# Memory's keys and values in an order written by hand, with one row of square sums per head; in prompt attention, maxima ahead of key scaling and queries ahead of keys

## The chip, the cores and the metric

The kernel is one program on one NeuronCore of a Trainium2 chip. The metric is the device time of one execution in microseconds (us); the time before is the median of three runs. The engines are named as in the profile: PE is TensorE's matmul, PEld its weight load, DVE is VectorE, ACT is ScalarE, POOL is GpSimd, SP is SyncE, which here only issues DMAs.

## The reference

One step of a decoder layer for two groups of requests, 1024 prompt tokens and 8 samples of 4 tokens, all in 32-bit floats:

```python
u, v, cq, ckv, kpe = split_in(rms_norm(x, g_mix) @ w_in)
a_out = chunk_gmlp(u, v, ...)                    # group A of the mixer
q = qk_rope(rms_norm(rms_norm(cq) @ w_uq))       # group B: 8 heads, 64 + 32 wide
k, vv = keys and values of the latents ckv_n     # prompt: own tokens; samples: 4096 cached ones
b_out = masked softmax attention of q over k, vv
x = x + concat(rms_norm(a_out), rms_norm(b_out)) @ w_o

hm = rms_norm(mem_prompt, g_mem_in)              # 256 memory tokens of 1024
mk = rms_norm((hm @ w_mk) per head of 128, g_mk) # 4 heads; an output of its own
mv = hm @ w_mv                                   # an output of its own
x = x + memory attention of x over mk, mv
x = x + conv_ffn(rms_norm(x))
```

## The kernel before

Everything is kept transposed, features on the 128 partitions and tokens along the row. A product of two 32-bit operands is made of three fast matmuls: each operand is split into a high part (a cast, usually on ACT, line 200 or 204 of `split`) and a low part (the remainder, usually on DVE, line 201 or 207), and `mm3` (line 185) sums high·high, low·high and high·low.

The program runs its stages one after the other: projections, prompt attention (`phase2a`), attention of the samples over cached pages (`phase2b`), memory's keys and values (`mem_kv`), output projection (`mixed`, `out_proj`), memory attention, feed-forward. Where a stage is inside a "manual schedule" of an engine, that engine runs its instructions in the order in which the code is written; elsewhere a scheduler orders them. `behind(a, b)` places instruction a after b.

**Prompt attention.** A unit is one head and one group of query tokens. `head_prep` transposes a head's keys and queries on PE (tiles `tp`) and splits them into `kTh`, `kTl` and `qTh`, `qTl`, 512 tokens at a time; `kT` holds 1024 tokens, in two halves written by two such preparations. `head_unit` takes scores (tiles `s`), their maxima on DVE (`pr`, `nm`), the exponential on ACT, transposes of the exponentials on PE and the sum over values (`o`). Rows of more than 512 keys are scored in two parts, the first over the first half of the row's keys. The scaling of the second 512 keys by their norms is two DVE instructions of `proj_group` (line 960).

**Memory's keys and values.** The raw memory tokens lie in two page buffers (`ck`). Before head 0, eight casts make their high parts `mh` and eight remainders `ml`. Four heads of keys follow (PSUM tile `b`, copies `kr`, squares `sq`), then values over four blocks of `w_mv` (PSUM tiles `v`). Sums over features, which normalise tokens and keys, are 12 matmuls with one column of ones:

```python
for h in range(4):
    for i in range(2):
        nc.tensor.matmul(st[:, 2 * h + i : 2 * h + i + 1], sq[h][:, i * P : i * P + P], self.ones[:, :1], ...)
```

The roots `r` then have a token per partition; to scale the keys they are spread over the partitions by eight matmuls, each of ones with a diagonal matrix that DVE makes of the identity (`diag`, lines 1657 and 1658). Between these lie the last softmax steps of the eighth sample batch (`batch_softmax`, list `late`; its roots are partly on POOL) and its sum over the cached values (`quad_pv`, tiles `o<-ck,S`).

**Output projection.** `mixed` loads `w_o` blocks and the mixer's outputs (`mix`, three chunks of 384, 384 and 288 tokens, split into `mx0`, `mx1`, `mx2`) through one ring of three `raw` buffers; `chunk(m, c)` multiplies block m of `w_o` with chunk c, adds the residual (`res`), stores it, and splits it into `xh`, `xl`, whose memory was that of `mem_kv`. `end` multiplies the samples' attention output `olT` by `w_uv`, and `mixed_sample` normalises it (`n`). SP issues the loads and stores of this stage in one queue.

Of the kernel before, what the change touches and what calls it, by code (L numbers as in the profile page):

```python
# [5 lines left out]
F32 = mybir.dt.float32  # L6
# [147 lines left out]
class Net:  # L154
# [83 lines left out]
    def rsqrt_steps(self, p, out, ss, scale, e=None, eps=EPS):  # L238
# [5 lines left out]
        x, q, y, a = (self.t(p, [P, n], d, f"rq{k}{n}", 2 if n < 100 else 1)[:w] for k, d in (("x", F32), ("h", F32), ("y", I32), ("a", F32)))  # L244
# [5 lines left out]
        for k in range(2):  # L250
            yield
            o = out if k else y
            if e is nc.vector:
# [6 lines left out]
                e.scalar_tensor_tensor(o, q, 5.0, y, ALU.add, ALU.mult)  # L260
# [411 lines left out]
    def phase2a(self):  # L672
# [80 lines left out]
        extra[2][:0] = preps[0][2:]  # L753
# [27 lines left out]
        with tc.manual_schedule(engines={E.PE, E.Activation, E.DVE, E.Pool}):  # L781
# [208 lines left out]
    def head_unit(self, p, pp, h, G, s, c):  # L990
# [7 lines left out]
        def scores(e):  # L998
# [9 lines left out]
            for z in range(nc_):  # L1008
# [3 lines left out]
                self.mm3(sv, [(qh[:, tq], ql[:, tq])], [(kh[:, kc], kl[:, kc])])  # L1012
# [166 lines left out]
    def phase2b(self):  # L1179
# [50 lines left out]
        at(last - 4, 3, lambda: self.split(*wk0, raws[0].rearrange("p (k n) -> p k n", k=8)))  # L1230
        for b in range(NB):
# [3 lines left out]
            for r, (k, pos) in enumerate(((12, 0), (13, 0), (14, 0), (14, 3) if b == NB - 1 else (15, 0), (15, 0) if b == NB - 1 else (15, 3), (16, 0), (17, 0), (17, 3), (18, 2), (19, 2), (20, 0), (21, 2), (22, 3))):  # L1235
                f = lambda b=b, r=r: self.batch_softmax(p, ppt, st[b], r, b == NB - 1)
                if n + k <= last:
                    at(n + k, pos, f)
                else:
                    late.append(f)  # L1240
# [15 lines left out]
        def steps(n0, n1):  # L1256
            for n in range(n0, n1):
# [27 lines left out]
                if 0 <= n < last:  # L1285
                    rope = (Q + 1, quads[Q + 1], st[(Q + 1) // 8]) if n % 2 and Q + 1 < NB * 8 else None
                    for f in self.pair_score(p, pp, n, quads[n // 2], st[n // 16], rope):
                        at(n + 1, -1, f)
# [12 lines left out]
        with tc.manual_schedule(engines={E.SP}):  # L1301
# [5 lines left out]
            mem = self.mem_kv(raws, wk0)  # L1307
            for f in late[:3]:
                f()
            next(mem)  # L1310
            steps(last + 1, last + 4)
            for _ in range(5):
                next(mem)
            steps(last + 4, last + 7)
            for f in late[3:]:
                f()
            for _ in range(6):
                next(mem)
            steps(last + 7, last + 16 + LAG)
            for _ in mem:  # L1320
                pass
# [140 lines left out]
    def batch_softmax(self, p, pp, s, r, final):  # L1462
# [28 lines left out]
        elif r == 4:  # L1491
            s["m"] = self.t(p, [P, 2, 32], F32, "mx", 2)
            peak(0, 0, 24)
        elif r == 5:
            s["it"] = norms(24, 32, nc.gpsimd if final else nc.vector)
# [6 lines left out]
        elif r == 8:  # L1502
            scale(nc.vector, 24, 32)
# [10 lines left out]
        elif r == 11:  # L1514
# [4 lines left out]
            if final:  # L1519
                self.less(nc.vector, s)  # L1520
# [20 lines left out]
    def batch_out(self, p, s, part, pp=None, final=False):  # L1541
        nc = self.nc
        if part == 0:
            s["oo"] = self.t(p, [P, 257], F32, "oo", 2)
            nc.scalar.copy(s["oo"], s["o"])
# [33 lines left out]
    def mem_kv(self, raws, wk0):  # L1579
# [7 lines left out]
        mh, ml = (self.t(p, [P, 8, 256], FR, x) for x in ("mh", "ml"))  # L1587
        acc = [self.t(p, [P, 256], F32, f"acc{z}") for z in range(2)]
        mr = [r.rearrange("p (k n) -> p k n", k=4) for r in raws[1:3]]
        xs = [(mh[:, k], ml[:, k]) for k in range(8)]  # L1590
        kr, sq = [], []

        for h in range(4):
            w = wk0 if h == 0 else self.stream(I["w_mk"][h], 8, raw=raws[3].rearrange("p (k n) -> p k n", k=8) if h == 1 else None)
            if h == 1:
                self.behind(self.cast, cast)
            yield
            ps = self.t(pp, [P, 512], F32, "b", 2)[:, :256]
            pairs = ((0, 0), (1, 0)), ((0, 1),)
            for z in pairs if h == 0 else (((0, 0), (0, 1)), ((1, 0),)):  # L1600
                for k in range(8):
                    if h == 0 and z is pairs[0]:
                        cast = self.split(*xs[k], mr[k // 4][:, k % 4], self.col("g_mem_in", k))
                    for a, e in z:
                        nc.tensor.matmul(
                            ps, w[a][:, k], xs[k][e], start=z[0] == (0, 0) and a + e + k == 0, stop=len(z) == 1 and k == 7
                        )
                    if h == 0 and z is pairs[0] and k % 2:
                        yield
# [988 lines left out]
```

## Time and profile before

| | us |
|---|---|
| three runs | 1813.99, 1815.08, 1815.76 |
| their median | 1815.08 |
| the profiled execution's own time | 1815.49 |
| its span (first to last instruction) | 1813.8 |
| PE busy in it | 1791.1 (99%) |
| DVE, ACT, POOL busy | 1347.4, 921.0, 705.9 |

Some 1.7 us lie outside the span. PE is busy nearly throughout, so a time is to be sought in PE's instructions and in the few places where it waits or runs at its lower clock.

### The profile page before, as it was taken

To read this page: it belongs to the slowest core of one execution; us is meant where nothing else is said; L and a number is where in the kernel's file an instruction comes from. 1 tells how busy PE (TensorE), PEld (TensorE's weight loads), DVE (VectorE), ACT (ScalarE), POOL (GpSimd) and SP (SyncE) were. 2 spreads that over 40 slices of the span, in tenths; PEclk is the share of its full clock that TensorE was granted. 3 is DMA by queue.
4 is the path that set the end of the run, shared out by engine and by line. 5 is a ranking of instruction groups with operands and counts; after the bars stand their busy time and mean duration, and the time that the engine had idled before them with its cause. 6 is when DMAs were issued, how large, how long until landed. Compare 5 with 4: busy or idle time off the path is not lost.

```text
span 1813.8 us, 39386 instructions
## 1 busy us (share of the span) xinstructions
PE 1791.1 (99%) x14259; PEld 1696.6 (94%) x14259; DVE 1347.4 (74%) x2778; ACT 921.0 (51%) x1931; POOL 705.9 (39%) x858
## 2 busy tenths in 40 slices
PE   9999999999999999999999999999999999999999
PEld 8999777769999999998899989999999999999999
DVE  7864777667678777787644678988888888878664
ACT  7335676766556555565434567433333333344442
POOL 1021656534455445453033001476677767400000
PEclk9999999999999999999999999999999999999999
DMA  8101354558876666663655255122222222584242
GB/s 324 48 18 62 118 184 129 164 164 229 226 206 191 190 186 194 178 190 125 188 157 195 97 169 181 58 95 83 72 71 83 72 83 83 163 319 150 88 147 78
DMA packets 153044, 261.06 MB, mean 144 GB/s; under 512 B 20881, under 2 KB 97394, under 8 KB 152850
## 3 DMA queue, kind: packets, MB, share of 16 engines
q1 hardware_dynamic: 151986, 257.50, 45.8%
q8 instruction: 113, 1.85, 0.5%
q10 hardware_dynamic: 864, 1.05, 0.2%
q14 instruction: 81, 0.66, 0.1%
HBM read 212.66 MB, written 45.82 MB: 143 GB/s over the span
## 4 chain that ended last, share of the span: by engine, by line
PE 77%; DVE 5%; ACT 2%; DMA 1%; issue 1%; POOL 1%; SPq 1%; DVEq 0%; ACTq 0%; POOLq 0%
PE s L185 22%; PE d L185 12%; PE b L185 8%; PE E L185 7%; PE F L185 7%; PE X L185 7%; PE A L185 3%; PE o L1046 2%; PE o L1537 2%; PE tp L1031 1%; PE tp L185 1%; PE s L1422 1%; PE tp L984 1%; PE v L185 1%; PE t L185 0%
## 5 line engine op out<-in xcount | busy, mean ns | idle before, releaser
L185 PE MATMUL s<-w2h,ch 128*128 128x256 f32 x1018 | 302.1, 297 | 0.0
L185 PE MATMUL s<-w2h,cl 128*128 128x256 f32 x1018 | 293.6, 288 | 0.0
L185 PE MATMUL s<-w2l,ch 128*128 128x256 f32 x1018 | 293.1, 288 | 0.0
L185 PEld LDWEIGHTS s<-w2h,ch 128*128 128x128 f32 x1018 | 191.6, 188 | 3.3 <-issue 2.9
L185 PEld LDWEIGHTS s<-w2h,cl 128*128 128x128 f32 x1018 | 191.4, 188 | 0.4 <-DVE rqa L257 0.4
L185 PEld LDWEIGHTS s<-w2l,ch 128*128 128x128 f32 x1018 | 191.8, 188 | 0.0
L1458 DVE TENSOR_REDUCE ss<-sq 128x16 f32<-128x1024 f32 x128 | 155.2, 1213 | 29.2 <-ACT sq L1455 29.1
L1407 POOL TENSOR_TENSOR cl<-cT,ch 128x512 fp32r<-128x512 f32 x64 | 86.2, 1346 | 197.8 <-ACT ch L1403 192.0
L1455 ACT ACTIVATE sq<-s 128x512 f32<-128x512 f32 x128 | 76.4, 597 | 72.3 <-PE s L185 72.2
L200 ACT CAST a<-brb 128x528 fp32r<-128x528 f32 x77 | 48.9, 634 | 114.7 <-PE d L185 111.2
L1452 ACT ACTIVATE sq<-s 128x512 f32<-128x512 f32 x128 | 76.6, 599 | 50.4 <-PE s L185 41.2
L201 DVE TENSOR_TENSOR a<-brb,a 128x528 fp32r<-128x528 f32 x77 | 54.3, 706 | 59.1 <-ACT a L200 58.8
L185 PE MATMUL d<-a,w 128*128 128x264 f32 x768 | 95.5, 285 | 1.2 <-DVE G L2366 1.2
L185 PEld LDWEIGHTS d<-a,w 128*128 128x128 f32 x768 | 94.3, 188 | 1.4 <-issue 1.4
L2233 POOL TENSOR_TENSOR lo<-s,hi 128x1024 fp32r<-128x1024 f32 x20 | 64.2, 3208 | 45.7 <-ACT hi L2232 45.7
L2289 ACT COPY a<-A 128x264 f32<-128x264 f32 x43 | 16.1, 375 | 120.6 <-PE A L185 114.3
L185 PE MATMUL mm<-wlo,xh 128*128 128x256 f32 (+3 forms) x272 | 77.1, 286 | 0.1
L185 PE MATMUL mm<-whi,xh 128*128 128x256 f32 (+3 forms) x272 | 77.1, 285 | 0.0
L185 PE MATMUL mm<-whi,xl 128*128 128x256 f32 (+3 forms) x272 | 76.9, 287 | 0.0
L1403 ACT CAST ch<-cT 128x512 fp32r<-128x512 f32 x128 | 73.6, 628 | 0.2 <-issue 0.2
L2355 POOL TENSOR_TENSOR cv<-cv,row 128x1056 f32<-128x1056 f32 x22 | 65.1, 2958 | 21.0 <-ACT cv L2354 21.0
L185 PE MATMUL d<-a,hi 128*128 128x264 f32 x552 | 72.0, 285 | 0.0
(802 smaller groups left out, 6371.3 us busy)
## 6 DMA issues: line engine op xcount, KB each, us to landing
cT<-cT SPq DMA_DIRECT2D x256, 160.0 KB, 2.7
ck<-ck SPq DMA_DIRECT2D x256, 144.0 KB, 3.5
raw<-w_up SPq DMA_DIRECT2D x44, 512.0 KB, 3.6
wsumd<-wsum SPq DMA_DIRECT2D x26, 512.0 KB, 3.5
actd<-cv SPq DMA_DIRECT2D x44, 264.0 KB, 2.4
brb<-actd SPq DMA_DIRECT2D x44, 264.0 KB, 5.6
wsum<-w_down SPq DMA_DIRECT2D x22, 512.0 KB, 3.7
raw<-wsumd SPq DMA_DIRECT2D x20, 512.0 KB, 3.7
```

Of the source, the lines that this page charges most:

```text
L185: x = self.nc.tensor.matmul(out, l, r, start=first and i == 0, stop=last and i == len(seq) - 1)
L200: first = {"act": nc.scalar.copy, "pool": nc.gpsimd.tensor_copy, "dve": nc.vector.tensor_copy}[eng](hi, src)
L201: low = lambda: nc.vector.tensor_tensor(lo, src, hi, ALU.subtract)
L1046: nc.tensor.matmul(u["o"][g : g + 64, o : o + m * P], s["v"][:, j, h % 4], th[:, z * P : (z + m) * P], start=j == 0, stop=b == len(banks) - 1,
L1403: nc.scalar.copy(d["h"][:, k], src[k])
L1407: (nc.vector if k else nc.gpsimd).tensor_tensor(d["l"][:, k], src[k], d["h"][:, k], ALU.subtract)
L1452: nc.scalar.activation(sq[:, 0], ps[:, :, n0 : n0 + 256], AF.Square)
L1455: nc.scalar.activation(sq[:, 1], pt.rearrange("p (e d) -> p e d", e=2), AF.Square)
L1458: yield lambda: nc.vector.tensor_reduce(s["ss"][:, g0 : g0 + 2].rearrange("p e (z h) -> p z e h", z=2), sq.rearrange("p z e (h d) -> p z e ...
L1537: nc.tensor.matmul(s["o"][j * 32 : j * 32 + 32], S[:, q * 4 + j], d["ck"][:, j, :257], start=q == 0 and j > 0, stop=q == 7)
L2233: eng.tensor_tensor(lo, src, hi, ALU.subtract)
L2355: nc.gpsimd.tensor_tensor(cv, cv, row, ALU.mult)
```

## The change

There are three parts.

**Prompt attention.** The two scalings of the second 512 keys move from the first unit's list to the second's, behind the maxima of the first unit's last two rows. For head 0, the transposes of those keys move behind those of the queries and of the exponentials. The three matmuls of a score are written out with kTl last instead of qTl.

**Memory's keys and values.** Order by hand on PE, ACT, DVE and SP, and: four of the eight splits are made one step ahead in free buffers (`mem_split`; tiles `S` and `ck`); the last batch's softmax roots move from POOL to DVE; sums over features become `st[32h : 32h + 32, :256]`, a row of 256 tokens per head over 32 partitions, eight matmuls with 32 columns of ones, and two one-column matmuls for the token norms of the values; DVE adds the token squares by three additions instead of two reductions; the roots are taken over that 128x256 tile in eleven DVE instructions; a broadcast is one matmul per head whose weights are a column of the identity, and the values' copies (`vf`) and stores come after the mixer's casts.

**Output projection.** PE and SP by hand for its first block: `chunk(0, 0)`, then the loads of the third mixer chunk (`rest`), `chunk(0, 1)`, then `end`.

```diff
@@ phase2a
-            extra[0][:0] = norm[4:]
-            extra[1][:0] = v1[3:]
-            steps, outs, pend, V = [], {}, [], []
+            extra[0][:0] = norm[4:5]
+            extra[1][:0] = norm[5:] + v1[3:]
+            steps, outs, pend, V = [], {3: [preps[0][2], self.flush]}, [], []
@@ head_unit
-                self.mm3(sv, [(qh[:, tq], ql[:, tq])], [(kh[:, kc], kl[:, kc])])
+                for i, (a, b) in enumerate(((qh, kh), (ql, kh), (qh, kl))):
+                    nc.tensor.matmul(sv, a[:, tq], b[:, kc], start=i == 0, stop=i == 2)
@@ phase2b
+        def mem_split():
+            hi = self.t(p, [P, 33, 32], FR, "S", 3).rearrange("p g m -> p (g m)")
+            lo = self.t(p, [P, 4, 288], FR, "ck", 15).rearrange("p k n -> p (k n)")
+            for k in range(4):
+                m0.append(tuple(x[:, k * 256 : k * 256 + 256] for x in (hi, lo)))
+                self.split(*m0[k], raws[1].rearrange("p (k n) -> p k n", k=4)[:, k], self.col("g_mem_in", k))
+        at(last - 1, 0, mem_split)
@@ mem_kv
+        head(0)
...
+        values(0, 0, 1)
...
+        acc = add()
...
+        values(2, 0, 1)
+        for z in range(2):
+            for h in range(4):
+                nc.tensor.matmul(
+                    st[32 * h : 32 * h + 32, :256], self.ones[:, :32], acc if z else sq[h], start=z == 0, stop=z == 1
+                )
         for i in range(2):
+            nc.tensor.matmul(st[:, 256 + i : 257 + i], acc[:, i * P : i * P + P], self.ones[:, :1], start=True, stop=True)
+        late[8]()
+        values(3, 0, 1)
+        for _ in self.rsqrt_steps(p, r, st[:, :256], 1.0 / 128, eps=EPS * EPS, room=sq):
+            pass
+        self.rows = self.root
+        self.rsqrt(p, rt, st[:, 256:258], 1.0 / (1024 * unit * unit))
+        seven()
         for i in range(2):
             vf = self.t(p, [P, 512], F32, "vf")
+            nc.scalar.activation(vf, av[i], AF.Copy, scale=rt[:, i : i + 1])
             nc.scalar.dma_start(O["o_mv"][i * P : i * P + P], vf)
+        for h in range(4):
+            nc.tensor.matmul(bc[h], self.ident[:, 32 * h : 32 * h + 1].broadcast_to([P, P]), r, start=True, stop=True)
+        for h in range(4):
+            nc.vector.scalar_tensor_tensor(kr[h], kr[h], self.col("g_mk"), bc[h], ALU.mult, ALU.mult)
+            nc.scalar.dma_start(O["o_mk"][h], kr[h])
@@ mixed
+                    if c:
+                        self.behind(self.cast, self.exp)
+                        self.behind(self.low, self.rows)
@@ out_proj
+        with self.tc.manual_schedule(engines={E.SP, E.PE}):
+            chunk(0, 0)
+            rest()
+            chunk(0, 1)
+            end()
```

What this does to the order of three engines' programs is shown at three places. PE in the first units of prompt attention, before: the four transposes of keys (`k`) come first, then those of queries (`q`), then those of exponentials (`pr`), and the first score of the next unit follows.

```order
1389 L984 MATMUL tp_2915<-ident_60,k_2594 96x128 x4
1390 L984 MATMUL tp_2923<-ident_60,q_2595 96x128 x4
1391 L1031 MATMUL tp_2939<-ident_60,pr_424_2849 128x128
1392 L1031 MATMUL tp_2939<-ident_60,pr_432_2878 128x128
1393 L1031 MATMUL tp_2939<-ident_60,pr_427_2857 128x128
1394 L1031 MATMUL tp_2939<-ident_60,pr_435_2886 128x128
1395 L185 MATMUL s_2949<-kTh_2709,qTh_2921 128x320
1396 L185 MATMUL s_2949<-kTl_2710,qTh_2921 128x320
1397 L185 MATMUL s_2949<-kTh_2709,qTl_2922 128x320
```

PE at the same place of the changed program:

```order
1389 L988 MATMUL tp_2917<-ident_60,q_2595 96x128 x4
1390 L1036 MATMUL tp_2932<-ident_60,pr_424_2849 128x128
1391 L1036 MATMUL tp_2932<-ident_60,pr_432_2875 128x128
1392 L1036 MATMUL tp_2932<-ident_60,pr_427_2857 128x128
1393 L1036 MATMUL tp_2932<-ident_60,pr_435_2883 128x128
1394 L988 MATMUL tp_2939<-ident_60,k_2594 96x128 x4
1395 L1017 MATMUL s_2949<-kTh_2709,qTh_2915 128x320
1396 L1017 MATMUL s_2949<-kTh_2709,qTl_2916 128x320
1397 L1017 MATMUL s_2949<-kTl_2710,qTh_2915 128x320
```

The key transposes have moved behind the exponentials, and in each score kTl is third instead of second.

SP's queue at the start of the output projection, before: `raw<-mix` are the mixer's loads, `res<-xT` residuals, `res_73<-res` stores of results, `raw<-w_o` blocks of weights.

```order
1298 L1764 DMA res_14901<-xT 128x384
1299 L1764 DMA res_14933<-xT 128x384
1300 L1764 DMA res_14971<-xT 128x384
1301 L1764 DMA res_15005<-xT 128x384
1302 L1734 DMA raw_14827<-mix_72 128x2x384
1303 L1734 DMA raw_14843<-mix_72 128x2x288
1304 L1734 DMA raw_14849<-mix_72 128x2x288
1305 L1734 DMA raw_14855<-mix_72 128x2x256
1306 L1768 DMA res_73<-res_14901 128x384
1307 L1734 DMA raw_14861<-mix_72 128x2x256
1308 L1764 DMA res_15071<-xT 128x288
1309 L1571 DMA raw_14965<-w_o 128x1024
```

The same place of the changed queue:

```order
1298 L1782 DMA raw_14791<-mix_72 128x2x384
1299 L1782 DMA raw_14797<-mix_72 128x2x384
1300 L1829 DMA res_73<-res_14820 128x384
1301 L1782 DMA raw_14855<-mix_72 128x2x288
1302 L1782 DMA raw_14861<-mix_72 128x2x288
1303 L1782 DMA raw_14867<-mix_72 128x2x256
1304 L1782 DMA raw_14873<-mix_72 128x2x256
1305 L1825 DMA res_14879<-xT 128x384
1306 L1825 DMA res_14937<-xT 128x384
1307 L1825 DMA res_14971<-xT 128x384
1308 L1581 DMA raw_14931<-w_o 128x1024
```

The first store of results now stands ahead of all four loads of the third chunk (128x2x288 and 128x2x256), and block 2 of `w_o` behind them and three residuals.

ACT around the values' copies and the stores of keys and values (`o_mv`, `o_mk`), before:

```order
960 L1667 ACTIVATE vf_14778<-v_2137_14618,rt_14667 128x512
961 L1670 DMA o_mv<-vf_14778 128x512
962 L204 ACTIVATE mx1h_14793<-raw_14809,cols_58 128x384 x2
963 L204 ACTIVATE mx1h_14793<-raw_14815,cols_58 128x384 x2
964 L204 ACTIVATE mx1h_14793<-raw_14821,cols_58 128x384 x2
965 L1545 COPY oo_14833<-o_14579 128x257
966 L1660 DMA o_mk<-kr_14451 128x256
967 L1660 DMA o_mk<-kr_14505 128x256
968 L1660 DMA o_mk<-kr_14540 128x256
969 L204 ACTIVATE mx1h_14793<-raw_14827,cols_58 128x384 x2
970 L1660 DMA o_mk<-kr_14575 128x256
971 L1562 COPY olT_5703<-m_14835 128x16x4
```

and in the changed program:

```order
962 L204 ACTIVATE mx1h_14756<-raw_14797,cols_58 128x384 x2
963 L1708 ACTIVATE vf_14724<-v_2101_14378,rt_14663 128x512
964 L1709 DMA o_mv<-vf_14724 128x512
965 L1708 ACTIVATE vf_14727<-v_2102_14379,rt_14663 128x512
966 L1709 DMA o_mv<-vf_14727 128x512
967 L1716 DMA o_mk<-kr_14443 128x256
968 L1716 DMA o_mk<-kr_14501 128x256
969 L1716 DMA o_mk<-kr_14537 128x256
970 L1716 DMA o_mk<-kr_14571 128x256
971 L1572 COPY olT_5703<-m_14768 128x16x4
972 L200 CAST xh_14807<-res_14820 128x384
```

Both copies and all six stores now stand between the last cast of `mx1h` and the copy `olT`, with which `end` begins, and ahead of the first cast of `xh`.

## Rows read from the trace of the kernel before

**Rows 1.** the page: busy us, share of the span and instructions by engine

```profile
PE 1791.1 (99%) x14259; PEld 1696.6 (94%) x14259; DVE 1347.4 (74%) x2778; ACT 921.0 (51%) x1931; POOL 705.9 (39%) x858
```

**Rows 2.** TensorE's waits: instruction, releaser, us in total, times, longest

```profile
PE b L1605 <- DVE S L1454: 1.5, 1, 1.5
...
PE b L1658 <- DVE diag L1657: 1.0, 3, 0.6
```

**Rows 3.** windows: start:end, length, busy us per engine, PEclk, DMA share, GB/s

```profile
215.60:222.50 6.90, 6.90 (x26) 5.28 (x25) 4.11 (x15) 0.99 (x2) 3.13 (x5) 0.51 0.59 199
...
871.00:874.40 3.40, 3.40 (x9) 2.65 (x9) 2.44 (x13) 1.08 (x1) 0.00 (x0) 0.50 0.44 118
...
893.00:960.00 67.00, 67.00 (x436) 66.45 (x435) 32.69 (x66) 25.88 (x57) 18.27 (x16) 1.00 0.54 166
```

**Rows 4.** timeline of PE, first prompt units: start, us, operation, idle before

```profile
213.46 0.41 PE L185 MATMUL s<-kTh,qTh 96*128 96x320 f32 x1 [0.99 <-ACT qTh L204]
```

**Rows 5.** timeline of DVE, same stretch

```profile
207.75 1.82 DVE L960 TENSOR_TENSOR k<-k,hr 128x512 f32<-128x512 f32 x2
```

**Rows 6.** timeline of ACT, same stretch

```profile
211.18 0.81 ACT L1023 ACTIVATE pr<-pr,nm,rq 128x512 f32<-128x512 f32 x1
...
212.72 0.69 ACT L204 ACTIVATE qTh<-tp,ggq 96x512 fp32r<-96x512 f32 x1
```

**Rows 7.** timeline of PE, head 0 and the start of head 1

```profile
848.06 0.36 PE L1605 MATMUL b<-mh,wk0h 128*128 128x256 f32 x1 [1.52 <-DVE S L1454]
...
852.34 0.28 PE L1605 MATMUL b<-mh,hi 128*128 128x256 f32 x1
852.45 0.28 PE L1605 MATMUL b<-ml,hi 128*128 128x256 f32 x1
```

**Rows 8.** timeline of ACT, casts of the memory tokens

```profile
846.79 3.31 ACT L204 ACTIVATE mh<-ck,cols 128x256 fp32r<-128x256 f32 x8
```

**Rows 9.** timeline of PE, column sums

```profile
867.92 0.95 PE L1636 MATMUL st<-ones,sq 128*128 128x1 f32 x8
...
869.60 1.03 PE L1639 MATMUL st<-ones,acc 128*128 128x1 f32 x8
```

**Rows 10.** timeline of PE, values of pages, broadcasts, start of the output projection

```profile
878.07 3.84 PE L1537 MATMUL o<-ck,S 128*32 128x257 f32 x61
...
881.84 1.36 PE L1658 MATMUL b<-diag,ones 128*128 128x128 f32 x8
...
885.83 0.42 PE L185 MATMUL b<-mx0h,hi 128*128 128x384 f32 x1
...
890.60 0.34 PE L185 MATMUL b<-mx1h,hi 128*128 128x384 f32 x1
...
893.99 1.97 PE L1328 MATMUL m<-wuv,olT 128*32 128x64 f32 x32
```

**Rows 11.** timeline of PE in memory attention: sums over 32 columns

```profile
1035.79 0.64 PE L1861 MATMUL st<-qsq,ones 128*32 128x256 f32 x8
```

**Rows 12.** timeline of DVE: a step of a root over 192 columns

```profile
840.44 0.36 DVE L259 SCALAR_TENSOR_TENSOR rqh<-rqa 128x192 f32<-128x192 f32 x1
```

**Rows 13.** timeline of DVE: a low part of weights

```profile
876.25 1.23 DVE L201 TENSOR_TENSOR lo<-raw,hi 128x1024 fp32r<-128x1024 f32 x1 [2.42 <-ACT hi L200]
```

**Rows 14.** timeline of ACT: the second copy of values

```profile
879.63 0.69 ACT L1667 ACTIVATE vf<-v,rt 128x512 f32<-128x512 f32 x1 [2.41 <-DMA o_mv<-vf]
```

**Rows 15.** DMA issues, 846 to 930 us: KB each, median us to landing

```profile
raw<-w_o SPq DMA_DIRECT2D x8, 512.0 KB, 3.9
...
raw<-mix SPq DMA_DIRECT2D x4, 384.0 KB, 3.7
...
o_mk<-kr ACTq DMA_DIRECT2D x4, 128.0 KB, 3.6
```

**Rows 16.** timeline of SP's queue: first store of results

```profile
892.06 0.40 SPq L1768 DMA_DIRECT2D res<-res  x1
```

**Rows 17.** timeline of PE: first use of w_o block 2

```profile
907.34 0.33 PE L185 MATMUL b<-mx0h,hi 128*128 128x384 f32 x1
```

More of the change, by code (lines that the diff above doesn't have):

```diff
@@ L1306, in phase2b @@
             self.wp = self.open("w", bufs=3, side="right")
[L1307 to L1321, printed above, removed]
+            six = [lambda n=n: steps(last + n, last + n + 1) for n in range(1, 7)]
+            self.mem_kv(raws, wk0, m0, late, six, lambda: steps(last + 7, last + 16 + LAG))
         self.close("p3")
@@ L1630, in mem_kv, with values @@
-        values(0)
-        yield
-        values(2)
-        yield
-        for h in range(4):
-            for i in range(2):
-                nc.tensor.matmul(st[:, 2 * h + i : 2 * h + i + 1], sq[h][:, i * P : i * P + P], self.ones[:, :1], start=True, stop=True)
+            nc.scalar.activation(sq[h], ps[h], AF.Square)
+        def values(j, *ii):
+            wh, wl = (pair(x) for x in w[j + 4])
+            for i in ii:
+                t = slice(i * P, i * P + P)
+                self.mm3(av[i], [tuple(x[:, t] for x in xs[2 * j + e]) for e in range(2)],
+                         [(wh[:, e], wl[:, e]) for e in range(2)], first=j == 0, last=j == 3)
@@ new lines, in add @@
+        def add():
+            q = [x.rearrange("p k n -> p (k n)") for x in mr]
+            for n in (1024, 512, 256):
+                x, y = q if n == 1024 else (q[0][:, :n], q[0][:, n : 2 * n])
+                nc.vector.tensor_tensor(q[0][:, :n], x, y, ALU.add)
+            return q[0][:, :256]
+        for f in six[:3]:
+            f()
+        for k in range(4, 8):
+            self.split(*xs[k], mr[1][:, k % 4], self.col("g_mem_in", k))
+        head(0)
+        late[0]()
+        load(1)
@@ new lines, in mem_kv @@
+        lows[1]()
+        load(2)
+        for f in six[3:5]:
+            f()
+        keep(0)
+        head(1)
+        late[1]()
+        lows[2]()
+        load(3)
+        for x in mr:
+            nc.scalar.activation(x, x, AF.Square, scale=unit)
+        late[2]()
+        late[3]()
+        late[4]()
+        lows[3]()
+        six[5]()
+        keep(1)
+        head(2)
+        load(4)
+        lows[4]()
+        self.peak()
+        keep(2)
+        head(3)
+        load(5)
+        keep(3)
@@ new lines, in mem_kv @@
+        values(0, 0, 1)
+        lows[5]()
+        late[4]()
+        load(6)
+        values(1, 0)
+        late[5]()
+        late[6]()
+        values(1, 1)
+        late[7]()
+        lows[6]()
+        acc = add()
+        load(7)
+        lows[7]()
+        self.less(nc.vector, self.final)
+        values(2, 0, 1)
[4 more added lines that the diff above has]
+                )
@@ L1773, in chunk @@
             self.square(self.pm, acc[c][:, :n], res, m)
-        end()
-        for m in range(10):
+        E = mybir.EngineType
+        with self.tc.manual_schedule(engines={E.SP, E.PE}):
+            chunk(0, 0)
+            rest()
+            chunk(0, 1)
+            end()
+        for m in range(1, 10):
             if m == 2:
```

152 lines of the change are left out of this document (67 added, 85 removed).

## The prediction

> **What bounds the kernel now.** The page comes first: PE is busy for 1791.1 us of a span of 1813.8 [rows 1], so the change can gain only from work that PE no longer does, from waits of PE, and from its clock. The list of PE's waits shows how little waiting there is; two of the places that the change rewrites stand in it, 1.5 us ahead of the first key head and 1.0 us in three pieces before the broadcasts [rows 2]. The windows give the granted clock: 0.51 for 6.9 us in the first prompt units, 0.50 for 3.4 us in memory's values, and 1.00 without a moment's idleness of PE from 893 to 960, the output projection [rows 3]. The last matters most for the price of the change: work that is delayed there meets a PE with no slack to give, and each wait lengthens the run.
>
> The change is costed stage by stage against the profiled execution (1815.49 us by its own time, 0.4 over the median of the three runs).
>
> **Prompt attention.** The two key scalings take 1.82 us on DVE ahead of the maxima of the unit's last two rows [rows 5]. The exponential of the last row starts at 211.18 and the queries' high part at 212.72, behind the keys' high part [rows 6]; PE's next score waited 0.99 us for it [rows 4]. With the scalings moved back, the exponentials on ACT follow one another without the DVE gap (about 0.3 us earlier), and the queries come ahead of the key cast: they are ready about 0.8 us earlier. The first half of a row's keys lies in the half of kT that was prepared before, so these scores need only the queries; the second half needs the new kTl, which is the last of each three. So the first half fills the time in which kTl is made, and the stage behind it starts 0.4 to 0.7 us earlier; I take 0.55. Against it: with qTl second instead of third the very first scores lose about 0.1, included. If the second half were to wait as long as before, it is 0. The transposes and most of the idleness stay, so I leave the half-clock stretch as it is.
>
> **Memory's keys and values.**
>
> *Head 0.* From the end of the wait, 848.06, to head 1 at 852.34 are 4.28 us, with the wait 5.80 [rows 2, 7]. At the step of head 1, 0.12 us [rows 7], 24 matmuls are 2.9 us; so 2.9 are lost, half in the wait and half because ACT makes a high part in 3.31 / 8 = 0.41 us [rows 8], and DVE's remainders follow. In the changed program eight matmuls have operands made one step earlier, 0.95 us of work, but the other four casts still come behind DVE's last sum of the scores, whose buffers they take over, and behind ACT's squares. I estimate a stall of 1.9 in place of 2.9, gain 1.0; bounds 0.3 (the casts are simply later) and 1.9 (only the pacing stays).
>
> *Sums.* The one-column matmuls are 24 records, 8 of them in 0.95 us and 8 in 1.03, with one small product between [rows 9]: 2.3 us go. Eight matmuls of 32 columns come in. Memory attention has the same form: eight records, which are four matmuls side by side, are over in 0.64 us [rows 11]; two such sets, overlapping like any matmuls, are 1.0 us. Two one-column matmuls stay, 0.45. Net gain 0.9.
>
> *Broadcasts.* From 881.84 to the output projection at 885.83 are 4.0 us [rows 10], 1.0 of it waiting for diagonals. Four matmuls of 256 columns replace eight of 128: the work itself stays about 1.8 us, restarts and waits go; gain 2.1. It needs the roots in time. Eleven instructions over 256 columns, by the 0.36 us for 192 [rows 12] some 0.45 with the gap, take 5.0 us on DVE; beside them PE has twelve 512-column matmuls (nine at half clock fill 3.40 us [rows 3], so 2.3 at full) and the 3.84 us of the pages' values [rows 10]. They are hidden by about 1 us. If the cover were gone, each microsecond would be paid in full.
>
> *Softmax of the last batch.* Its last maximum goes to another place; by the DVE work ahead of it, 0.25 us more waiting.
>
> *Clock.* The fall to 0.50 at 871.0 follows directly on the stretch of one-column matmuls, in which PE was hardly ever idle. Nine 512-column matmuls then ran in 3.40 us [rows 3]. With the columns gone I expect the clock to hold: 1.7 us gained. The Trainium skill (TensorE: Matmul & The Clock Gate, Part 1) describes the gate as closing after idleness and opening after sustained activity. By that rule the one-column stretch would not have cost the clock, the cause of the 871 us fall would lie elsewhere, and the 1.7 us would not be gained. The row speaks for the columns, since no idleness stood there; the rule is kept as a rival.
>
> So the stage gives 1.0 + 0.9 + 2.1 - 0.25 = 3.75, and 1.7 by the clock.
>
> **Output projection.** T is its first matmul (885.83 before). What is handed on late is paid here, in four places.
>
> First, mx1. Its PSUM bank is one that the broadcasts used, free when DVE has scaled the four kr. Before those, DVE has the roots (ending about 2 us before T), then the low part of w_o's second block, 1.23 [rows 13], and only this frees the third mixer load's buffer. The load lands 3.7 us after issue [rows 15], then come cast, remainders and four kr: about T + 6. mx1 is wanted 4.8 after T [rows 10]. Wait 1.4, bounds 0 and 2.
>
> Second, olT. It stands on ACT behind all mx1h, two vf and six stores. The fourth mixer load puts the last mx1h near T + 5; vf takes 0.69 and the second waits 2.41 for the first store's landing, since there is one vf buffer [rows 14]. Copy and stores end near T + 10.6. The product with w_uv was at T + 8.2 before [rows 10] and is at T + 9.6 with the first wait. Wait 1.0, bounds 0 and 1.2.
>
> Third, w_o block 2. Before, its load passed the queue with all third-chunk loads but one ahead of the first store, which was at T + 6.2 [rows 16]; now all four follow that store. Also xl, on memory of the kr, waits until the last o_mk has landed, 3.6 us after its issue [rows 15], and the third chunk's remainders are queued behind xl on DVE, as are its buffers behind them. T + 10.6 + 3.6 + 1.7 for four remainders, a load, three residuals: block 2 is issued near T + 17, lands 3.9 later [rows 15], and is split by T + 23.2 (a cast, then 1.23 for the low part [rows 13]). It was wanted at T + 21.5 before [rows 17], now at about T + 23.1. Wait 1.0; 0 if the DMAs keep their medians, 3.5 if three in a row are 1 us slower.
>
> Fourth, n, whose roots run between the same DVE instructions: 0.6, bounds 0 and 1.1.
>
> Together 4.0, bounds 0 and 7.8.
>
> **Sum.** -0.55 - 3.75 - 1.7 + 4.0 = -2.0 us: 1813.5 by the profiled execution, **1813.1** by the median. A run of this kernel can hardly be told from no change within 0.2%, 3.6 us.
>
> **Rivals.**
>
> *The delays are hidden.* If the loads land early and the stores of o_mk release their memory at once, the projection gives back at most 1.5 to 2. Then -6.0 + 1.75 = -4.2, 1810.9. For it: before, every wait of this stage was covered, so the slack may be more than the rows show. Against: T itself moves up by some 6 us, while the DMAs do not get faster.
>
> *Slower: block 2 of w_o comes late.* The chain o_mv, o_mk, xl, third chunk, w_o holds four landings in series. It decides from the point at which the projection's waits pass 6.0 us, about 1 us more per landing than the medians. At 7.8 and with half a clock stretch of 3.4 us after the waits (1.7 each, one or two), the sum is +3.5 to +5.2: 1818.6 to 1820.3, centre 1819.2.
>
> *The clock is not won.* Either the fall in the values stays, or the projection's waits, which stand near one another as those at 213 to 215 us did [rows 4], bring one like it. Then -2.0 + 1.7 = -0.3: 1814.8.
>
> *The first clock loss goes too.* The prompt units wait less; if the 6.9 us at 0.51 [rows 3] are run at full clock, 3.4 more are gained: -5.4, 1809.7. Against: their transposes and half the idleness stay.
>
> **Chances.** Forecast 0.42, hidden delays 0.20, clock not won 0.18, slower 0.12, first clock loss gone 0.08. Likeliest time 1813.1, its own range 1811.5 to 1815 by the middle halves of its bounds. The range that leaves out no more than 2 in 10 runs from 1809.3, taking in most of hidden delays, to 1817.5, short of the slow rival. Faster by over 0.2% (below 1811.5) is most of hidden delays, the first clock loss and a little of the forecast: 0.30. Slower by over 0.2% (above 1818.7) is most of the slow rival: 0.10. Between: 0.60.
>
> **What would show it.** Right: the next stage of the prompt units about 0.5 us earlier; no granted clock of 0.5 between 860 and 890; the output projection starting some 6 us earlier, then waits of PE for DVE kr, for ACT olT, and around w_o's block 2, of about 4 us in all. Wrong: broadcasts that wait for DVE's roots; a first score that waits as before; an output projection without waits (then faster), or waits beyond 6 us (then slower).

## The result, and the profile after

The changed kernel takes 1817.10 us, median of 22 runs (1813.64 to 1822.29), against 1814.95 for the kernel before, also 22 runs (1810.29 to 1819.02): a ratio of 1.0017, 95% interval 1.0011 to 1.0024. It is some 3 us slower where 2 us less were forecast. The profiled execution of after has an own time of 1815.88 us and a span of 1814.2, only 0.4 above that of before. So the two profiles show why nothing is won; what makes the other executions slower still, they don't show. The profiled execution of after also spent less time at half clock in the first prompt units, 3.41 us for 6.83; whether that is chance is taken up below.

The page of after: PE is busy 2.8 us less than before [rows 1], and the kernel isn't faster by that.

```profile
PE 1788.3 (99%) x14247; PEld 1693.4 (93%) x14247; DVE 1348.8 (74%) x2777; ACT 921.4 (51%) x1931; POOL 700.6 (39%) x844
```

So two stages are to be read apart: what lies ahead of the output projection, and the projection itself. PE's timeline of after, from head 0 to the projection's first matmul, is to be read against [rows 7, 9, 10]:

```profile
843.29 0.28 PE L1620 MATMUL b<-S,wk0h 128*128 128x256 f32 x1
...
845.55 0.38 PE L1620 MATMUL b<-mh,wk0h 128*128 128x256 f32 x1 [1.15 <-ACT mh L204]
...
848.17 0.36 PE L1620 MATMUL b<-S,hi 128*128 128x256 f32 x1
...
866.30 0.64 PE L1692 MATMUL st<-sq,ones 128*32 128x256 f32 x8
866.75 0.61 PE L1692 MATMUL st<-ck,ones 128*32 128x256 f32 x8
867.30 0.61 PE L1696 MATMUL st<-ones,ck 128*128 128x1 f32 x4
...
870.99 3.84 PE L1547 MATMUL o<-ck,S 128*32 128x257 f32 x61
874.76 1.99 PE L1713 MATMUL b<-sq,ident 128*128 128x256 f32 x8
...
876.73 0.42 PE L185 MATMUL b<-mx0h,hi 128*128 128x384 f32 x1
```

The wait ahead of head 0 has become one of 1.15 within it, the sums are three short groups, the broadcasts follow the pages' values without a wait, and the projection starts at 876.73 instead of 885.83: 9.1 us earlier.

Its last matmul with the high part `mx2h`, however, starts at 980.95, where it was 981.05 before, and so all is lost again. PE's waits in after from 840 to 960 say where (instruction, releaser, us in total, times, longest):

```profile
PE m L1331 <- ACT olT L1572: 1.5, 1, 1.5
PE o L1812 <- ACT n L1809: 1.4, 1, 1.4
PE b L185 <- ACT hi L200: 1.2, 1, 1.2
PE b L1620 <- ACT mh L204: 1.2, 1, 1.2
PE b L185 <- DVE kr L1715: 0.7, 1, 0.7
PE b L185 <- DVE lo L201: 0.6, 1, 0.6
```

And windows of after, with the columns of [rows 3]:

```profile
215.60:222.50 6.90, 6.90 (x43) 4.58 (x42) 5.19 (x18) 4.02 (x9) 3.81 (x6) 1.00 0.53 156
232.11:235.52 3.41, 3.41 (x16) 2.18 (x16) 1.95 (x10) 0.25 (x1) 1.66 (x2) 0.50 0.72 248
871.00:874.40 3.40, 3.40 (x65) 2.03 (x58) 3.19 (x9) 0.00 (x0) 0.00 (x0) 1.00 0.23 85
...
904.54:911.37 6.83, 6.14 (x21) 6.08 (x22) 1.87 (x6) 2.51 (x7) 1.00 (x1) 0.50 0.61 200
...
893.00:960.00 67.00, 63.75 (x378) 62.81 (x377) 31.70 (x63) 23.84 (x53) 18.58 (x16) 0.95 0.55 168
```

PE waits five times in a stage that had no wait before (from 893 to 960 it is busy for 63.75 of 67 us, for 67.00 before), and a stretch of 6.83 us at half clock, 1.2 GHz, lies where there was none. The fall at 871 is gone. The one in the first prompt units is 3.41 us long in this execution, at 232, and was 6.83, at 215; it comes and goes between executions (below).

Where the five waits lie, and what DVE and ACT did ahead of them, shows the chain. PE's timeline of after first:

```profile
882.16 0.41 PE L185 MATMUL b<-mx1h,hi 128*128 128x384 f32 x1 [0.66 <-DVE kr L1715]
...
888.13 1.97 PE L1331 MATMUL m<-wuv,olT 128*32 128x64 f32 x32 [1.53 <-ACT olT L1572]
...
901.37 0.44 PE L185 MATMUL b<-mx0h,hi 128*128 128x384 f32 x1 [1.16 <-ACT hi L200]
...
902.63 0.44 PE L185 MATMUL b<-mx0h,lo 128*128 128x384 f32 x1 [0.64 <-DVE lo L201]
...
905.23 0.63 PE L1812 MATMUL o<-ident,n 32*128 32x32 f32 x4 [1.45 <-ACT n L1809]
```

DVE's timeline of after in the same stretch, with the remainder `xl` that waited for the stores of keys, and the two halves of n's root (lines 250 to 264 of `rsqrt_steps`) around a low part:

```profile
890.45 0.56 DVE L201 TENSOR_TENSOR xl<-res,xh 128x384 fp32r<-128x384 f32 x1 [6.90 <-DMA o_mk<-kr]
...
898.32 0.14 DVE L264 SCALAR_TENSOR_TENSOR rqy<-rqh,rqy 32x1 f32<-32x1 f32 x1
901.35 1.23 DVE L201 TENSOR_TENSOR lo<-raw,hi 128x1024 fp32r<-128x1024 f32 x1 [2.89 <-ACT hi L200]
902.50 0.96 DVE L259 SCALAR_TENSOR_TENSOR rqa<-rqy 32x1 f32<-32x1 f32 x1
...
904.21 0.15 DVE L264 SCALAR_TENSOR_TENSOR r<-rqh,rqy 32x1 f32<-32x1 f32 x1
```

ACT's timeline of after, with the second copy of values, olT, the cast of block 2 and n:

```profile
884.33 0.69 ACT L1708 ACTIVATE vf<-v,rt 128x512 f32<-128x512 f32 x1 [2.11 <-DMA o_mv<-vf]
...
887.86 0.21 ACT L1572 COPY olT<-m 128x64 f32<-128x64 f32 x1 [2.84 <-issue]
...
900.28 1.04 ACT L200 CAST hi<-raw 128x1024 fp32r<-128x1024 f32 x1 [3.30 <-DMA raw<-w_o]
...
904.46 0.72 ACT L1809 ACTIVATE n<-raw,r 32x512 f32<-32x512 f32 x1 [2.29 <-DVE r L264]
```

And SP's queue in after, with the residuals' loads and that of block 2:

```profile
892.30 1.41 SPq L1825 DMA_DIRECT2D res<-xT  x3
893.83 0.36 SPq L1581 DMA_DIRECT2D raw<-w_o  x1
```

Block 2 of w_o is issued at 893.83 and its cast starts at 900.28. Its low part stands on DVE in the midst of the root for n (898.32, then 902.50 to 904.21): DVE stands idle for 2.89 us behind a load with half a root undone, and n, which needs nothing of w_o, comes after it.

### The profile page after: what moved, and what is told of

It is laid out like the page before. It is cut to its first block, busy times and chain, and to the rows that moved or that the text cites. A ratio compares the mean times of both kernels' runs of the same rounds, so it can differ in the third digit from the quotient of the medians.

```text
span 1814.2 us, 39352 instructions
## 1 busy us (share of the span) xinstructions
PE 1788.3 (99%) x14247; PEld 1693.4 (93%) x14247; DVE 1348.8 (74%) x2777; ACT 921.4 (51%) x1931; POOL 700.6 (39%) x844
## 3 DMA queue, kind: packets, MB, share of 16 engines
q10 hardware_dynamic: 864, 1.05, 0.2%
## 4 chain that ended last, share of the span: by engine, by line
PE 77%; DVE 4%; ACT 3%; DMA 2%; issue 1%; SPq 1%; ACTq 0%; DVEq 0%; POOL 0%
PE s L185 20%; PE d L185 12%; PE b L185 7%; PE E L185 7%; PE F L185 7%; PE X L185 7%; PE A L185 3%; PE s L1017 2%; PE o L1051 2%; PE tp L1036 1%; PE o L1547 1%; PE tp L185 1%; PE s L1425 1%; PE tp L988 1%; PE v L185 1%
```

## The experiments

Each ratio is to the kernel before, run beside it on the same chip; e1 and e11 start from the kernel before, all others from the changed one.

**Two parts of the change alone.** In e1 the kernel before gets the prompt part; in e2 the changed kernel loses it.

```diff
 e1, on the kernel before (e2 takes the same lines back from the changed one)
-        extra[2][:0] = preps[0][2:]
+        extra[2][:0] = preps[0][3:]
...
-            extra[0][:0] = norm[4:]
-            extra[1][:0] = v1[3:]
-            steps, outs, pend, V = [], {}, [], []
+            extra[0][:0] = norm[4:5]
+            extra[1][:0] = norm[5:] + v1[3:]
+            steps, outs, pend, V = [], {3: [preps[0][2], self.flush]}, [], []
...
-                self.mm3(sv, [(qh[:, tq], ql[:, tq])], [(kh[:, kc], kl[:, kc])])
+                for i, (a, b) in enumerate(((qh, kh), (ql, kh), (qh, kl))):
+                    nc.tensor.matmul(sv, a[:, tq], b[:, kc], start=i == 0, stop=i == 2)
```

> The kernel before with the change's prompt attention alone (key scaling behind the maxima, queries ahead of keys, kTl last in a score). Theory 1 (the scores' half over the first keys no longer waits): the stages behind the first units start 0.5 to 0.7 us earlier, and nothing else differs, so 0.5 faster, hardly to be told. Theory 2 (the clock is what moves): the half-clock stretch of 6.8 us there shrinks to 3.4 as in the profile of the whole change, 1.7 more, so 2.2 us faster than before. Rival (the gain of 2.25 seen at the start of the page attention is lost again later, at a wait that does not depend on PE): page attention starts 2 us earlier and ends at the same time as before.

> The whole change without its prompt attention: the rewritten keys and values of the memory and the output projection alone. Theory 1 (the stages add up): the output projection starts 6.9 us earlier than before instead of 9.1, the waits in it are the same 5.4 us, and the time is 0.5 to 2.2 us above that of the whole change. Theory 2 (the delays in the projection hang on DMAs that do not come earlier with PE): the waits shrink by what PE comes later, and the time is that of the whole change within 0.5 us.

e1: 1813.21 us, ratio 0.9996 [0.9986, 1.0006]. e2: 1817.9, ratio 1.0020 [1.0009, 1.0031]. The prompt part costs nothing and may gain about 1 us; the loss is all in memory's keys and values with the projection behind them. In e1's profile the prompt units have no stretch at half clock at all, and the gain is not lost again later: the projection starts and ends 4.8 us earlier than before.

**The copies and stores ahead of olT.** e3 gives vf a second buffer, so that the second copy no longer waits for the first store.

```diff
-            vf = self.t(p, [P, 512], F32, "vf")
+            vf = self.t(p, [P, 512], F32, "vf", 2)
```

> The whole change with two buffers for the values' copies instead of one. Theory 1 (stores in series: the second copy waits 2.1 us for the first store, the four key stores stand behind it, and xl waits for their landing, which holds the third chunk and block 2 of w_o): the wait for olT goes (1.5 us), xl starts 2 us earlier, the waits around block 2 (3.2 us) shrink by 2, in all 3 us faster, more if the half-clock stretch at 904 goes too. Theory 2 (SP's order holds block 2: its load stands behind the first store of results, the third chunk and three residuals): olT's wait goes, block 2 is as late as now relative to the start of the projection, and its waits grow by what PE comes earlier; the time is the same within 1 us.

e3: 1815.7 us, ratio 1.0009 [0.9999, 1.0019]. The wait for olT is gone, but PE then comes to block 2 sooner than its load does. In PE's timeline of e3 the wait for the cast is 2.33 where it was 1.16:

```profile
899.19 0.45 PE L185 MATMUL b<-mx0h,hi 128*128 128x384 f32 x1 [2.33 <-ACT hi L200]
...
900.45 0.44 PE L185 MATMUL b<-mx0h,lo 128*128 128x384 f32 x1 [0.64 <-DVE lo L201]
...
903.04 0.63 PE L1812 MATMUL o<-ident,n 32*128 32x32 f32 x4 [1.45 <-ACT n L1809]
```

The window of e3 at half clock:

```profile
901.53:908.36 6.83, 5.38 (x20) 5.25 (x20) 2.63 (x10) 2.59 (x7) 1.00 (x1) 0.50 0.74 211
```

So the waits are in series: what one gives up, the next one takes.

**The token root's place.** In e4 and e6 vf has two buffers and the root `rt`, which in the changed kernel is drawn out on DVE between the remainders of mx1 up to 880.3 and so delays the four kr, is made ahead of time: in e4 on POOL, in e6 step by step between the steps of the key root.

```diff
 e4
+        it = self.rsqrt_steps(p, rt, st[:, 256:258], 1.0 / (1024 * unit * unit), nc.gpsimd)
...
-        self.rsqrt(p, rt, st[:, 256:258], 1.0 / (1024 * unit * unit))
 e6 (fine: one step at a time)
+        one = self.rsqrt_steps(p, rt, st[:, 256:258], 1.0 / (1024 * unit * unit), fine=True)
+        for _ in self.rsqrt_steps(p, r, st[:, :256], 1.0 / 128, eps=EPS * EPS, room=sq, fine=True):
+            next(one)
...
```

> The whole change with the token norms' root taken on GpSimd, started ahead of the keys' roots, and two buffers for the values' copies; the copies and then the keys' scaling and stores need not stand behind that root's eleven small steps on DVE any more. Theory 1 (late scaling and stores are the cause): keys are scaled about 3 us earlier, the copies some 6 us earlier, xl waits for no store; the waits for kr and olT go and those around block 2 shrink to under 1 us, 5 us faster than the whole change, and 8 if the half-clock stretch that follows those waits goes with them: 1809 to 1812. Theory 2 (SP's order): kr's and olT's 2.2 us go, the 3.2 us around block 2 stay or grow; 0 to 2 us faster.

> The whole change with the eleven steps of the token norms' root placed one by one between the eleven of the keys' roots on DVE, and two buffers for the values' copies. As with that root on GpSimd, the copies and stores no longer stand behind it, but without the 1.2 us that PE waited there for oo behind the copies. Theory 1: kr's and olT's waits go, xl comes 3 us earlier; the keys' roots end 1 us later and just make the broadcasts. Theory 2: the waits around block 2 of w_o stay at about 3 us with the half-clock stretch behind them, as they did with the root on GpSimd. By both about 3 us faster than the whole change, 1 us faster than with the root on GpSimd; if the waits around block 2 go as well, theory 2 falls.

e4: 1813.66 us, ratio 0.9999 [0.9987, 1.0011]; e6: 1813.67, ratio 0.9993 [0.9981, 1.0005]. In both the waits for kr and olT are gone. Those around block 2 and n stay (0.82, 0.65 and 1.46 in e6), and so does a stretch at half clock. In e4 PE also waits 1.21 us for `oo` just ahead of the projection, which e6 doesn't have.

**The queue of loads.** e5 puts the third chunk's loads ahead of the first store again; e7 does that together with e6.

```diff
-            chunk(0, 0)
-            rest()
+            chunk(0, 0, rest)      # rest() between the residual's sum and the store
```

> The whole change with SP's four loads of the third mixer chunk ahead of the first store of results instead of behind it; on DVE three pairs of that chunk's remainders then come ahead of xl. Theory 2 (SP's order holds block 2 of w_o): the third chunk lands 3 to 4 us earlier, block 2 likewise, the waits around it (3.2 us) go, the half-clock stretch behind them too: 5 to 6 us faster than the whole change. Theory 1 (the chain of late copies, stores and xl): the first two loads come earlier, but the fourth needs a buffer and block 2 a store of results that hang on xl, which still waits for the key stores; olT's 1.5 us and kr's 0.7 us stay in any case; 0 to 2 us faster.

> Both edits together: token norms' root between the keys' roots with two copy buffers, and the third chunk's loads ahead of the first store. If the two causes are in series, as the two traces with one of them removed suggest, only this one frees block 2 of w_o: all six waits of the projection are under 1.5 us in sum, no half-clock stretch follows them, and the gain ahead of the projection (about 8 us) is kept: 1806 to 1809. If the half-clock stretch comes without the waits, 1810 to 1812. If neither edit is the cause, 1813 or more.

e5: 1817.36 us, ratio 1.0014 [1.0005, 1.0024]: by itself the order of the queue wins nothing; the waits for block 2 and olT become shorter, those for kr (2.12) and n (1.78) longer. e7: 1814.07, ratio 0.9992 [0.9981, 1.0004], not the 1806 to 1809 expected. In e7 block 2 is in time and one wait is left, 1.78 us for n; 1.4 us after it the clock falls all the same. PE's timeline of e7:

```profile
899.25 0.43 PE L1824 MATMUL o<-ident,n 32*128 32x32 f32 x4 [1.78 <-ACT n L1821]
```

The window of e7 behind it, PEclk at 0.50:

```profile
900.61:904.02 3.41, 3.41 (x12) 3.41 (x11) 0.75 (x3) 0.76 (x3) 0.49 (x1) 0.50 0.68 210
```

**The wait for n.** e8 is e7 with the low part of block 2 behind the whole root of n; e9 also puts n's scaling ahead of block 2's cast on ACT.

```diff
+                if m == 1:
+                    self.cast2, self.low2 = self.cast, self.low
...
+        self.behind(self.low2, self.root)                                              # e8, e9
-        nc.scalar.activation(n, self.b_s, AF.Copy, scale=r)
+        self.behind(self.cast2, nc.scalar.activation(n, self.b_s, AF.Copy, scale=r))   # e9
```

> The kernel of e7 with one order more: on DVE the low part of w_o's block 2 comes behind the whole root of the mixed sample's norm, whose last two steps it parted in e7 (PE waited 1.78 us there for n). The computation is the same. Theory 'waits' (what the change gives back in the output projection is PE's waits and the half-clock stretch that follows them): n still stands on ACT behind the cast of block 2, so the wait for n falls to about 0.8 us at a place three matmuls earlier; 0.9 us less than e7 in the projection, and the ratio to before near 0.9985. Rival 'clock alone' (the projection's stretch at half clock comes anyway in this place, with the work and not with the waits): the stretch near 900 us stays, 3.4 us long, and mx2's last matmul keeps its 974.5 us within 1 us.

> The kernel of e8 with n's scaling also ahead of the cast of w_o's block 2 on ACT. The computation is the same. Theory 'waits': the wait for n is gone or under 0.2 us, one of about 0.5 us for the cast takes its place, all of the projection's waits together are under 0.8 us; with no wait over 0.6 us no half-clock stretch follows between 890 and 945 us, so mx2's last matmul comes 1.2 us earlier than in e7 by the waits and 1.7 more by the clock: 971.6 against 974.52, and the ratio to before is 0.9970 to 0.998. Rival 'clock alone': the stretch at half clock stays near 900 us without a wait ahead of it, mx2's last matmul near 973.3, ratio 0.9985.

e8: 1812.84 us, ratio 0.9984 [0.9975, 0.9993]. Its wait for n didn't shrink to 0.8; it is 2.34. ACT's timeline of e8 shows why: the cast ahead of n stood 3.35 us for the load, and n behind it.

```profile
897.55 1.04 ACT L200 CAST hi<-raw 128x1024 fp32r<-128x1024 f32 x1 [3.35 <-DMA raw<-w_o]
...
899.34 0.70 ACT L1822 ACTIVATE n<-raw,r 32x512 f32<-32x512 f32 x1
```

e9: 1808.04 us in six runs, ratio 0.9958 [0.9946, 0.9969], over 7 us under the kernel before, the best of all, and more than was expected. One wait of 0.74 is left and the clock doesn't fall in the projection, which goes against the rival 'clock alone'. The window of e9:

```profile
893.00:960.00 67.00, 66.26 (x413) 65.84 (x413) 31.79 (x63) 24.99 (x55) 22.23 (x19) 1.00 0.57 174
```

**The same two orders without the rest.** e10 puts the two orders of e9 into the changed kernel, e11 into the kernel before.

> The changed kernel with the two orders of e9 alone: the mixed sample's root whole on DVE ahead of the low part of w_o's block 2, and n's scaling ahead of its cast on ACT. One vf, the token root behind the key roots and the first store ahead of the third chunk's loads stay as the change has them. The computation is the same. Theory 'last wait' (the half-clock stretch follows the wait for n and the ones just before it): the waits for kr (0.7) and olT (1.5) stay, one of some 1.2 us for block 2 stays, those for lo (0.6) and n (1.45) go; the output projection from its first matmul to mx2's last takes 2.1 us less by the waits (104.2 now, 95.2 in the kernel before) and 1.7 to 3.4 less by the clock: 98.7 to 100.4, ratio to before 0.9990 to 1.0000. Rival 'all the waits' (the three that stay are enough to bring the clock down): 102.1, ratio 1.0005 to 1.0010.

> The kernel before with the two orders of e9 alone. The computation is the same. Theory 'repair' (e9 is fast because the change's own gain ahead of the projection is no longer given back there, and its orders are worth nothing without the change): PE waited for nothing between 893 and 960 us in the kernel before, so there is nothing to win; the projection takes 95.2 us as before, ratio 0.9995 to 1.0005. Rival 'the orders gain by themselves': ratio under 0.9985, and then the change is not what made e9 fast.

e10: 1813.65 us, ratio 0.9998 [0.9989, 1.0007]. The waits for kr and olT stay, those for n and block 2 are 0.5 each, that for lo is gone: 3.3 us in all, and the clock holds. PE's waits of e10 from 840 to 960:

```profile
PE m L1331 <- ACT olT L1572: 1.5, 1, 1.5
...
PE b L185 <- DVE kr L1715: 0.7, 1, 0.7
PE o L1813 <- ACT n L1810: 0.5, 1, 0.5
PE b L185 <- ACT hi L200: 0.5, 1, 0.5
```

The window of e10, PEclk at 1.00:

```profile
893.00:960.00 67.00, 65.95 (x413) 65.61 (x412) 31.43 (x64) 25.33 (x56) 22.15 (x19) 1.00 0.57 181
```

e11: 1815.34 us, ratio 1.0007 [0.9996, 1.0018]. In the kernel before the orders win nothing, as there was no wait to take away. So e9's gain is the change's own, no longer given back. (e9's other orders, the two copies and the place of the token root, were not tried on the kernel before; PE has no wait in its projection that they could take.)

**All of them side by side.** For each profiled execution: the output projection from its first matmul (mx0) to the start of the last mx2h one, PE's waits in it, the length at half clock in it, and what 95.2 us (its length without waits, as before) plus the waits plus half of that length would make.

| | length | waits | at half clock | sum |
|---|---|---|---|---|
| before, e1, e11 | 95.2, 95.2, 95.2 | 0 | 0 | 95.2 |
| after | 104.2 | 5.4 | 6.8 | 104.1 |
| e2 | 101.9 | 4.5 | 3.4 | 101.4 |
| e3 | 103.6 | 5.1 | 6.8 | 103.7 |
| e4 | 101.6 | 3.0 | 6.8 | 101.6 |
| e5 | 103.6 | 6.0 | 3.4 | 102.9 |
| e6 | 100.4 | 2.9 | 3.4 | 99.9 |
| e7 | 99.2 | 1.8 | 3.4 | 98.7 |
| e8 | 99.4 | 2.3 | 3.4 | 99.3 |
| e9 | 96.4 | 0.7 | 0 | 96.0 |
| e10 | 99.0 | 3.3 | 0 | 98.5 |

Waits and clock leave at most 0.7 us of any length unexplained. The medians of the runs follow the table only roughly, since stretches at half clock also come and go elsewhere: in the first prompt units they are 0 (e1, e3, e4, e7, e10, e11), 3.41 (after, e6, e8, e9) or 6.83 us long (before, e2, e5). The long one stands in one of ten profiles with the prompt part (e5) and in two of three without it.

## Why the prediction was wrong

The time, 1817.10, lies just inside the stated range, which went up to 1817.5; that is the range's width and no merit of the reasoning, for the change slows the kernel where a gain of 2 us was forecast.

**Ahead of the projection the mechanism was right, the size low.** 6.0 us were predicted, 9.1 measured. The prompt stage gives 2.25 of these, for 0.55 predicted, but the shorter stretch at half clock is in that. Executions without such a stretch compare better. From a wait at the start of the prompt units to one near their end PE takes 176.59 us in e11, without the prompt part, and 175.88 in e1, with it (PE's timelines of e11, then of e1):

```profile
199.14 0.33 PE L185 MATMUL s<-kTh,qTh 96*128 96x128 f32 x1 [0.19 <-ACT qTh L204]
...
375.73 0.76 PE L1031 MATMUL tp<-ident,pr 128*128 128x128 f32 x5 [1.10 <-ACT pr L1023]
```

```profile
198.63 0.33 PE L1013 MATMUL s<-kTh,qTh 96*128 96x128 f32 x1 [0.20 <-ACT qTh L204]
...
374.51 0.76 PE L1032 MATMUL tp<-ident,pr 128*128 128x128 f32 x5 [1.10 <-ACT pr L1024]
```

In e3, e4, e7 and e10, also with it and without the stretch, it is 175.2 to 175.8. So the part gives some 0.7 to 1.4 us by itself. Whether the shorter stretch of after is chance or partly the change's stays open: over the runs the mean granted clock of e1 is 0.9983 (12 runs), of the kernel before beside it 0.9971 (35 runs), which speaks for a share of the change, while the prediction left the stretch as it was and had its end only as a rival, at 0.08. Page attention behind it ends another 0.5 earlier; nothing was predicted there, and the runs don't tell why. From the pages' last score to head 1 it is 1.45 (6.68 before, 5.23 after) for 1.0, to the end of the values 2.9 for 2.35 (sums, softmax and clock together), and 2.0 for the broadcasts' 2.1. The roots were hidden as forecast, by about 1 us: they end at 873.8 on DVE, the broadcasts start at 874.76 and wait for nothing.

**The fall at 871** is gone, as predicted: none of the ten profiles with the new sums (after, e2 to e10) has a granted clock of 0.5 between 846 and 900. Of the three with the old sums two have it at 871 or 872; in e1 it came at 845, just behind PE's 1.52 us wait for the softmax. The profiles speak for the one-column sums or for what stood around them; no run here parts these. The prediction kept as a rival the rule that the gate closes after idleness (the Trainium skill, TensorE: Matmul & The Clock Gate, Part 1); as it read the rule, the columns would not have mattered. In the projection the rows go the rule's way: the falls of e7 and e8 follow idleness of 1.78 and 2.34 us, though not every such wait is followed by one (last section).

**The step that failed is the output projection's give-back, "Together 4.0, bounds 0 and 7.8".** It measures 9.0: waits of 5.4, 3.4 for the clock (half of 6.83 us) and 0.2 that stay open. By its terms:

- First, mx1: 1.4 predicted, 0.66 measured. The four kr end 5.3 us after the projection's start, not 6.
- Second, olT: 1.0 predicted, 1.53 measured. Copy and stores end 11.1 us after the start, not 10.6; the six stores' issues alone take 3.1 on ACT.
- Third, block 2: 1.0 predicted, 1.16 + 0.64 measured. Its issue was foreseen to the tenth (17 us after the start, measured 17.1). The landing wasn't: the cast starts 6.4 after the issue, and 3.9 was taken from the median of [rows 15]. By the prediction's own sum, 23.2 against 23.1, the wait would have been 0.1; the 1.0 was an allowance for late loads, and too small. The median of the eight w_o loads in this stretch is 4.9 in the changed kernel.
- Fourth, n: 0.6 predicted, 1.45 measured. That its "roots run between the same DVE instructions" was seen, but not that the low part, waiting for a load, would stand in the midst of the root.
- The clock. "With the columns gone I expect the clock to hold" was true only of the place where it fell before. A fall brought by the projection's waits stood only among the rivals and is not in the 4.0; 6.83 us at half clock came in this execution, twice the 3.41 that went.

The runs show which waits bring it. In e10 those for kr and olT are as in after, and the clock holds; in e7 and e8 n alone is late, by 1.78 and 2.34, and the clock falls. So it is the last group, block 2's high and low part and n, 3.25 us of waits within 5 in after and 1.05 in e10. All eight profiles in which one of these waits is over 1 us (after, e2 to e8) have a fall between 900 and 909, the two others with the change's sums (e9, e10) have none. n's wait is enough, by e7 and e8. Block 2's two seem to be enough as well: in e3 the clock falls at 901.53, behind waits of 2.33 and 0.64, when that for n is only beginning (1.45 long, up to 903.04).

With that group all but gone the projection is 5.2 us shorter in the profiles (104.2 to 99.0), the larger part of the 9.0. In the runs the ratio goes from 1.0017 to 0.9998, about 3.4 us, and from there to e9's 0.9958 it is 7 more, of which the projections of the two profiles show 2.6 (99.0 to 96.4). What the rest is, single profiles don't show. The slower rival had this place, with too high a bar: it "decides from the point at which the projection's waits pass 6.0 us", and together with the clock 5.4 were enough.

Over the runs, the mean granted clock of the changed kernel is 0.9970 (22 runs), of the kernel before 0.9971 (101 runs beside the experiments), of e10 0.9986 (11) and of e9 0.9990 (6). So what the change wins of the clock ahead of the projection is spent in it, and e10 and e9 keep it, in more than the one execution profiled.

## What to carry to other kernels

A gain ahead of a stage in which the bounding engine has no slack is worth what that stage's loads, copies and roots can follow; list what it wants next, in order, with the time at which each is handed on, and look for short chains of dependent instructions that a scheduler has parted by one that waits for a DMA. Waits in such a stage are in series, so taking away one shows little until the last is gone (e3, e5), and a wait that brings the clock down counts for half the stretch that follows as well. Where a change makes one part faster and the whole slower, a few lines of order at the receiving end may be the remedy: two of them alone bring the changed kernel back to the time before (e10), and with the second copy buffer, the token root and the loads in their new places as well it is 0.42% under it (e9).

## What had not been expected of the hardware

PE's clock often falls in the profiles behind a single wait in an otherwise busy stretch: behind 1.78 us in e7 and 2.34 in e8, and in e9 and e11 also in page attention, at 498 and 500 us, at the end of waits of 1.75 and 2.33 (PE's timeline of e11, then its window):

```profile
499.73 0.40 PE L185 MATMUL s<-w2h,cl 128*128 128x288 f32 x1 [2.33 <-DVE cl L1407]
```

```profile
500.17:503.58 3.41, 3.41 (x18) 3.41 (x17) 3.34 (x7) 1.83 (x5) 1.56 (x2) 0.50 0.68 186
```

But the 1.5 us for olT at 888 brought none in after or e10, nor did the 1.52 at 848 in the kernel before, while the same wait did in e1. Longer ones decide no better. In the feed-forward, between 1580 and 1589 us, PE waits for the tile `G` of DVE in every profile: 2.04 us in e3, 1.76 in e5 and 2.14 in e10 brought a fall, 1.83 in e2 and 2.25 in e6 none, and neither did the 2.12 for kr in e5. In the 13 profiles there are twelve waits of over 1.7 us, and at nine of them the clock falls, at the latest 2.4 us behind their end. So a wait of 1.5 to 2.3 us may or may not cost 1.7 us more, from one execution to the next, and a forecast has to carry both.
